# A 64-byte tile ahead of the retention heads' turned output

## The chip, the core and the metric

The kernel runs on one NeuronCore of a Trainium2 chip. Its engines work side by side, each with its own instruction queue: TensorE (PE in the profile, with its weight loads listed apart as PEld), VectorE (DVE), ScalarE (ACT) and GpSimd (POOL); SyncE (SP) only issues DMAs. SBUF, the on-chip memory, has 128 partitions, and a tile of shape [128, ...] takes the same bytes in every partition. PSUM receives what TensorE computes. The metric is the device time of one execution in microseconds; of several executions the median is given.

## What is computed

One layer of a decoder trunk on 512 tokens and 16 learned meta tokens, D = 1024. One input projection feeds a retention branch (4 heads, values 512 wide) and a GLA branch (4 heads, values 256 wide); each branch is projected back to 1024 columns, weighted by a learned sigmoid gate and added; an output projection, the residual and a final RMS norm follow. Cut to what matters here:

```
u = rms_norm(h, norm_gain)
(rq, rk, rv, rg, gq, gk, gv, gg, glr, m_ret, m_gla) = jnp.split(u @ w_in, points, axis=-1)
o_ret = retention_chunked(rope(rq), rope(rk) * RET_QK_DIM ** -0.5, rv)
o_ret = head_group_norm(o_ret, ret_norm_gain) * jax.nn.silu(rg)
...
merged = jax.nn.sigmoid(m_ret) * (o_ret @ w_branch_ret) + jax.nn.sigmoid(m_gla) * (o_gla @ w_branch_gla)
h = h + merged @ w_out
return rms_norm(h, final_norm_gain)[:, N_META:]
```

The part that the change touches is `o_ret @ w_branch_ret`: per head a [1024 x 512] by [512 x 512] product.

## The kernel before

**Numbers in two parts.** Every matrix is held as a high and a low part in float32r (`hi` by a ScalarE cast, `lo` by a VectorE subtraction, both in `split`, L154), and a product is three matmuls: high by high, high by low, low by high (`mm3`, L188 to L193). In `nc.tensor.matmul(out, a, b)` the second argument `a` is the stationary operand, loaded into the array as weights ahead of the matmul, and `b` is the moving operand, streamed through it. The profile names them in the other order: `br_p<-oh,br_h` is the result, the moving tile, the stationary tile.

**Projections.** `quad` computes a pair of column blocks by a Strassen-like scheme of seven products of 24 matmuls each, mostly 256 columns wide; its matmuls are on L318. Weights come by DMA into six raw buffers, are split, and are held in three `hi` and three `lo` buffers of the pool `wp`.

**Retention heads.** For each head h the program runs `ret_qk`, `ret_g`, `ret_v`, `ret_scores` and `ret_attention(h)`. The last computes the four row blocks (`values`, `av` in the profile), norms and gates them, and turns them with TensorE transposes: `turn` (L478 to L493) writes the turned output, scaled by a gain, as the tiles `oh` (ScalarE, L491) and `ol` (VectorE, L492), each [128, 4, 512]. They are taken on L1331 and L1332: for heads 0, 1 and 2 from the pool `rp` under the tags `oh` and `ol` (one buffer each, so the three heads use the same bytes one after the other), for head 3 from the pool `cp`.

**Who reads them.** `branch` (L463 to L476) multiplies heads 0 and 1 with their rows of `w_branch_ret`: eight column blocks, in each 4 row blocks x 3 = 12 matmuls with 512 columns, 96 in a head. They alternate with the products of `quad` for the gate `mg` (`turns`, L1450). `ret_branches` (L1415 to L1441) takes heads 2 and 3 together, in two halves; in each half come first 48 matmuls of head 2 and then 48 of head 3, which add to the same PSUM banks. In all of them `oh` or `ol` is the moving operand and a `hi` or `lo` buffer the stationary one. Later the tags `oh` and `ol` hold `fgb` and `hs[1]` (L1491, L1492), which no matmul reads.

**Order.** Each engine's order is not simply that of the source: the build sorts instructions by when they are ready in its own estimate, with a few orders fixed by hand (`after`, `pin`). Waits between engines and for a buffer that becomes free are put in by the framework.

**Where tiles lie.** The built program gives each tile a byte offset in the partition. The last column is the offset's remainder by 128, which is 0 or 64 for all of these:

| tile | operand of | offset | mod 128 |
|---|---|---|---|
| `oh`, heads 0 to 2 | `br`, moving | 212,864 | 0 |
| `ol`, heads 0 to 2 | `br`, moving | 221,056 | 0 |
| `oh`, head 3 | `br`, moving | 4,800 | 64 |
| `ol`, head 3 | `br`, moving | 22,208 | 64 |
| the six `hi` and `lo` buffers of `wp` | `br`, stationary | 102,848 to 123,328 | 64 |
| `vh`, `vl` | `av`, moving | 173,952, 182,144 | 0 |
| `sh`, `sl` | `av`, stationary | 198,528, 203,648 | 0 |
| `ga12` (GLA branch) | `bg_a`, moving | 149,632 | 0 |
| fourth sum of `merged` (high, low) | last `wo_b`, stationary | 52,672, 70,080 | 64 |

Rows within these tiles lie multiples of 128 bytes apart, so the remainder holds for every matmul of the groups named. `oh` and `ol` of heads 0 to 2 are the last tiles of `rp`: `ol` ends at 229,248 of 229,376 bytes. Where `oh` begins, the GLA stage had held `ga22h` (tag `gQ`), a matmul operand of its last branch product.

Of the kernel before, what the change touches and what calls it, by code (L numbers as in the profile page):

```python
# [21 lines left out]
F32 = mybir.dt.float32  # L22
# [6 lines left out]
P = 128  # L29
# [79 lines left out]
def hybrid_kernel(ctx: ExitStack, tc: tile.TileContext, I, out: bass.AP):  # L109
    nc = tc.nc  # L110
# [39 lines left out]
    def pat(name):  # L150
        return pa.tile([P, 512], F32, tag="pa", name=name)
# [36 lines left out]
    def mm3(o, lh, ll, rh, rl, first, last, dense=False):  # L188
        m = nc.tensor.matmul(o, lh, rh, start=first, stop=False)  # L189
        if dense:  # L190
            pin(m)
        nc.tensor.matmul(o, lh, rl, start=False, stop=False)  # L192
        m = nc.tensor.matmul(o, ll, rh, start=False, stop=last)  # L193
        if dense:
            order[:] = [m]

    def rstd_of(x, n, rows, name, eps=EPS):
        v = sp.tile([P, 1], F32, tag="rv", name=f"{name}_v")
        r = sp.tile([P, 1], F32, tag="rr", name=f"{name}_r")
        nc.vector.tensor_scalar(v[:rows], x, 1.0 / n, eps, op0=ALU.mult, op1=ALU.add)  # L200
        R["pow"] = nc.gpsimd.tensor_tensor(r[:rows], v[:rows], mhalf[:rows], op=ALU.pow)
        return r
# [275 lines left out]
    def turn(src, half, oh, ol, gain, gcol, name):  # L478

        for e2 in range(2):  # L480
            pt = pat(f"{name}_{half}{e2}")
            for e in range(2):
                for b in range(2):
                    nc.tensor.transpose(pt[:, (2 * e + b) * P:(2 * e + b + 1) * P],
                                        src[:, 2 * half + b, (2 * e2 + e) * P:(2 * e2 + e + 1) * P], ident)
            for e in range(2):
                k = 2 * e2 + e
                g = gain[:, gcol + k:gcol + k + 1]
                v = pt[:, 2 * e * P:(2 * e + 2) * P]
                h = oh[:, k, half * 256:(half + 1) * 256]  # L490
                nc.scalar.activation(h, v, AF.Copy, scale=g)  # L491
                nc.vector.scalar_tensor_tensor(ol[:, k, half * 256:(half + 1) * 256], v, g, h.bitcast(F32),  # L492
                                               op0=ALU.mult, op1=ALU.subtract)  # L493
# [701 lines left out]
    rp = ctx.enter_context(tc.tile_pool(name="rp", bufs=1, reuse_waits="tile"))  # L1195
# [6 lines left out]
    def tmp(name):  # L1202
        return rp.tile([P, 2 * HT], F32, tag="tmp", name=name, bufs=7)[:, :512]
# [122 lines left out]
    def ret_attention(h):  # L1326
        sh, sl, sm = R["s", h]
        vh, vl = R["v", h]
        vm, sg = R["vm", h], R["sg", h]

        oh, ol = [(rp if h < 3 else cp).tile([P, 4, T], F32R, tag=f"o{n}" if h < 3 else f"x{n}0", name=f"o{n}{h}")  # L1331
                  for n in "hl"]  # L1332
        R["o", h] = oh, ol

        def values(ib):
            ps = pat(f"av{h}{ib}")
            for jb in range(ib + 1):
                o = SOFF[jb] + (ib - jb) * P
                mm3(ps, sh[:, o:o + P], sl[:, o:o + P], vh[:, jb, :], vl[:, jb, :], jb == 0, False)
            nc.tensor.matmul(ps, sm[:, ib * P:(ib + 1) * P], vm, start=False, stop=True)  # L1340
            b6 = sp.tile([P, 6], F32, tag="b6", name=f"b6{h}{ib}")
            mv = sp.tile([P, 2], F32, tag="mv", name=f"mv{h}{ib}")
            nc.vector.bn_stats(b6, ps)
            nc.vector.bn_aggr(mv, b6)
            r = rstd_of(mv[:, 1:2], 1.0, P, f"g{h}{ib}")
            nm = sp.tile([P, 1], F32, tag="nm", name=f"nm{h}{ib}")
            nc.vector.scalar_tensor_tensor(nm, mv[:, 0:1], -1.0, r, op0=ALU.mult, op1=ALU.mult)
            on = tmp(f"on{h}{ib}")
            nc.scalar.activation(on, ps, AF.Identity, scale=r, bias=nm)
            nc.vector.tensor_mul(sg[:, ib, :], on, sg[:, ib, :])  # L1350

        for ib in range(NTB):
            values(ib)
            R["pow", h] = R["pow"]
            yield
        if h < 2:
            yield
        for half in range(2):
            turn(sg, half, oh, ol, rgain, h * 4, f"ot{h}")
            yield  # L1360
# [82 lines left out]
    for h in range(4):  # L1443
        if h == 0:
            drain(ret_qk(h))
        else:
            at = ret_attention(h - 1)
            weave(ret_qk(h), at if h < 3 else islice(at, NTB + 1))
        if h % 3:
            weave(turns(gates_gla(h - 1), ret_branch(h - 1)), ret_rope(h), skip=2)  # L1450
            weave(ret_g(h), ret_scores(h))
            drain(ret_v(h))
        else:
            weave(run(ret_g(h), ret_v(h)), run(every(ret_rope(h), 3, 2, at if h else None), ret_scores(h)))
    weave(gates_ret(), ret_attention(3))

    mh, ml = [[cp.tile([P, 4, T], F32R, tag=f"x{n}1", name=f"m{n}0"),
# [150 lines left out]
```

## Time and profile before

| | |
|---|---|
| median of 3 runs (lowest, highest) | 763.93 us (763.68, 764.01) |
| span of the profiled execution | 762.2 us |
| busy share: PE, PEld, DVE, ACT, POOL | 98%, 92%, 80%, 59%, 17% |
| granted TensorE clock, mean | 0.996 |
| DMA | 116.89 MB, 153 GB/s on the mean |

The profiled execution's own time is not given apart from its span; between the span and the median lie 1.7 us. A PE row's duration includes the pipeline, so neighbouring matmuls overlap in the profile; how fast they follow each other is read from the starts of rows, or from a piece of the chain of waits, which counts each stretch of time once. The windows below name times from the span's start.

### The profile page before, as it was taken

The page shows a single profiled execution, that of the slowest core. Times are in us where ns is not written, and L with a number is a line of the kernel's source. Part 1 is how long each engine was busy: PE and PEld are TensorE (multiplying, and loading weights), DVE is VectorE, ACT ScalarE, POOL GpSimd, SP SyncE. Part 2 cuts the span into 40 slices and gives each one's busy share as a digit, 9 for nine tenths or more (in the row PEclk, how much of TensorE's full clock was granted, in tenths as well). Part 3 has the DMA queues.
Part 4 walks back from the last instruction along what each step waited for, and adds up shares of the span by engine and source line. Part 5 has one row for each costly group of instructions (what it writes and reads, how often), then busy time and mean ns, then how long its engine had stood idle before and what let it go on. Part 6 is the DMA issues. An engine that isn't in the chain of part 4 may idle for free.

```text
span 762.2 us, 14057 instructions
## 1 busy us (share of the span) xinstructions
PE 750.4 (98%) x5595; PEld 701.5 (92%) x5595; DVE 611.2 (80%) x873; ACT 451.2 (59%) x764; POOL 133.4 (17%) x172
## 2 busy tenths in 40 slices
PE   9999999999989999999999999999999999999996
PEld 6799899999989999998889999889999999988996
DVE  6799877689897799778957688876787989775994
ACT  7897584666974465545646455555554756532562
POOL 2211200112231122110330100240002210111142
PEclk9999999999999999999999999999999999999999
DMA  9864321822568973753684563696477357687503
GB/s 301 277 146 106 89 84 45 185 82 70 137 168 229 295 171 91 164 144 119 176 239 125 117 161 111 166 206 154 120 166 159 93 148 193 227 196 199 136 29 111
DMA packets 99995, 116.89 MB, mean 153 GB/s; under 512 B 5717, under 2 KB 90837, under 8 KB 99673
## 3 DMA queue, kind: packets, MB, share of 16 engines
q1 hardware_dynamic: 79896, 88.19, 37.8%
q0 software_dynamic: 19744, 27.27, 19.6%
q8 instruction: 44, 0.72, 0.4%
q10 hardware_dynamic: 288, 0.53, 0.2%
q14 instruction: 23, 0.18, 0.1%
HBM read 104.44 MB, written 11.53 MB: 152 GB/s over the span
## 4 chain that ended last, share of the span: by engine, by line
PE 87%; DVE 9%; issue 2%; ACT 1%; POOL 0%; POOLq 0%; DVEq 0%
PE rv_b L318 6%; PE rg_b L318 6%; PE rqk_b L318 5%; PE rqk_c L318 4%; PE br_p L192 4%; PE br_p L193 3%; PE br_p L189 3%; PE gg_b L318 3%; PE mr_b L318 3%; PE gv_p L640 3%; PE rv_c L318 3%; PE bg_b L318 3%; PE rg_c L318 3%; PE mg_b L318 2%; PE gg_c L318 2%
## 5 line engine op out<-in xcount | busy, mean ns | idle before, releaser
L192 PE MATMUL br_p<-ol,br_h 128*128 128x512 f32 x128 | 50.6, 395 | 1.7 <-DVE ol L492 1.7
L189 PE MATMUL br_p<-oh,br_h 128*128 128x512 f32 x128 | 50.4, 394 | 0.0
L193 PE MATMUL br_p<-oh,br_l 128*128 128x512 f32 x128 | 50.3, 393 | 0.0
L154 ACT CAST rv_h<-rv_w 128x1024 fp32r<-128x1024 f32 x24 | 25.2, 1052 | 26.9 <-DVE rv_w L371 9.6
L154 DVE TENSOR_TENSOR rv_l<-rv_w,rv_h 128x1024 fp32r<-128x1024 f32 x24 | 29.3, 1221 | 9.2 <-ACT rv_h L154 9.2
L154 DVE TENSOR_TENSOR rg_l<-rg_w,rg_h 128x1024 fp32r<-128x1024 f32 x20 | 24.4, 1219 | 8.4 <-ACT rg_h L154 8.4
L192 PEld LDWEIGHTS br_p<-ol,br_h 128*128 128x128 f32 x128 | 24.0, 188 | 7.4 <-DVE ol L492 2.4
L154 ACT CAST br_h<-br_w 128x1024 fp32r<-128x1024 f32 x16 | 16.8, 1050 | 23.4 <-PE br_p L192 9.9
L282 POOL DMA_DIRECT2D rqk_x<-in_w_in_dram x8 | 10.4, 1305 | 109.5 <-DVE vl L154 66.2
L193 PEld LDWEIGHTS br_p<-oh,br_l 128*128 128x128 f32 x128 | 24.0, 188 | 5.5
L154 ACT CAST rg_h<-rg_w 128x1024 fp32r<-128x1024 f32 x20 | 21.0, 1052 | 13.2 <-PE br_p L192 5.0
L189 PEld LDWEIGHTS br_p<-oh,br_h 128*128 128x128 f32 x128 | 24.0, 188 | 5.1 <-ACT oh L491 0.2
L318 PE MATMUL rv_b<-rv_l,fh 128*128 128x256 f32 x96 | 27.1, 282 | 0.1
L318 PE MATMUL rqk_b<-fh,rqk_h 128*128 128x256 f32 (+1 forms) x96 | 27.2, 283 | 0.0
L318 PE MATMUL rqk_b<-fh,rqk_l 128*128 128x256 f32 (+1 forms) x96 | 27.1, 282 | 0.0
L318 PE MATMUL rqk_b<-fl,rqk_h 128*128 128x256 f32 (+1 forms) x96 | 27.1, 282 | 0.0
L154 DVE TENSOR_TENSOR rqk_l<-rqk_w,rqk_h 128x1024 fp32r<-128x1024 f32 x20 | 24.4, 1220 | 3.3 <-ACT rqk_h L154 3.3
L318 PE MATMUL rg_b<-rg_h,fl 128*128 128x256 f32 x96 | 27.0, 281 | 0.0
L318 PE MATMUL rv_b<-rv_h,fl 128*128 128x256 f32 x96 | 27.0, 281 | 0.0
L318 PE MATMUL rg_b<-rg_h,fh 128*128 128x256 f32 x96 | 26.9, 281 | 0.0
L318 PE MATMUL rg_b<-rg_l,fh 128*128 128x256 f32 x96 | 26.9, 281 | 0.0
L318 PE MATMUL rv_b<-rv_h,fh 128*128 128x256 f32 x96 | 26.9, 280 | 0.0
(720 smaller groups left out, 3239.4 us busy)
## 6 DMA issues: line engine op xcount, KB each, us to landing
rv_w<-in_w_in_dram SPq DMA_DIRECT2D x16, 512.0 KB, 4.2
br_w<-in_w_branch_ret_dram SPq DMA_DIRECT2D x16, 512.0 KB, 3.5
rqk_w<-in_w_in_dram SPq DMA_DIRECT2D x12, 512.0 KB, 4.5
rg_w<-in_w_in_dram SPq DMA_DIRECT2D x12, 512.0 KB, 5.4
rqk_x<-in_w_in_dram SPq DMA_DIRECT2D x8, 512.0 KB, 5.3
rqk_x<-in_w_in_dram POOLq DMA_DIRECT2D x8, 512.0 KB, 8.1
rg_x<-in_w_in_dram SPq DMA_DIRECT2D x8, 512.0 KB, 4.2
rg_x<-in_w_in_dram POOLq DMA_DIRECT2D x8, 512.0 KB, 7.7
```

The costliest lines, as they stand in the source:

```text
L154: return nc.scalar.copy(hi, src), nc.vector.tensor_sub(lo, src, hi.bitcast(F32))
L189: m = nc.tensor.matmul(o, lh, rh, start=first, stop=False)
L192: nc.tensor.matmul(o, lh, rl, start=False, stop=False)
L193: m = nc.tensor.matmul(o, ll, rh, start=False, stop=last)
L282: x = nc.gpsimd.dma_start(t, block(0, 1), accum_op=ALU.add)
L318: m = nc.tensor.matmul(ps[t][:, :n] if wide else ps[t], l, r, start=first and j == 0, stop=kk == 3 and j == 2, skip_group_check=not fresh ...
L640: m = nc.tensor.matmul(pss[t], (al if j == 1 else ah)[t // 2, kh][:, k, c], (lo if j == 2 else hi)[:, kk, :], start=q == kk == j == 0, sto ...
```

## The change

Ahead of the two tiles of head 0, a tile of 16 floats, 64 bytes in each partition, is taken from the same pool and set to zero on GpSimd. Nothing reads it. Tiles of a pool follow one another in the order in which their tags first appear, so `oh` begins at 212,928 and `ol` at 221,120 for heads 0, 1 and 2 (remainder 64 by 128), and `ol` ends at 229,312. No other tile moves.

```
         vm, sg = R["vm", h], R["sg", h]
 
+        if h == 0:
+            nc.gpsimd.memset(rp.tile([P, 16], F32, name="gap"), 0.0)
         oh, ol = [(rp if h < 3 else cp).tile([P, 4, T], F32R, tag=f"o{n}" if h < 3 else f"x{n}0", name=f"o{n}{h}")
                   for n in "hl"]
         R["o", h] = oh, ol
```

More of the change, by code (lines that the diff above doesn't have):

```diff
@@ L1329, in ret_attention @@
         vm, sg = R["vm", h], R["sg", h]
+        if h == 0:
+            nc.gpsimd.memset(rp.tile([P, 16], F32, name="gap"), 0.0)
         oh, ol = [(rp if h < 3 else cp).tile([P, 4, T], F32R, tag=f"o{n}" if h < 3 else f"x{n}0", name=f"o{n}{h}")
```

## The prediction, made before the result was known

> **What bounds the kernel now.** I read the page's busy shares first, then its chain of waits, then the groups.
>
> ```profile
> span 762.2 us, 14057 instructions
> ...
> PE 750.4 (98%) x5595; PEld 701.5 (92%) x5595; DVE 611.2 (80%) x873; ACT 451.2 (59%) x764; POOL 133.4 (17%) x172
> ...
> PE 87%; DVE 9%; issue 2%; ACT 1%; POOL 0%; POOLq 0%; DVEq 0%
> ...
> L192 PE MATMUL br_p<-ol,br_h 128*128 128x512 f32 x128 | 50.6, 395 | 1.7 <-DVE ol L492 1.7
> L189 PE MATMUL br_p<-oh,br_h 128*128 128x512 f32 x128 | 50.4, 394 | 0.0
> L193 PE MATMUL br_p<-oh,br_l 128*128 128x512 f32 x128 | 50.3, 393 | 0.0
> ```
>
> TensorE is busy for 98% of the span and holds 87% of the chain that ended last. So what counts is how closely its matmuls follow each other. The three `br` groups are the only matmuls that read the moved tiles: 3 x 128, of which heads 0, 1 and 2 have 288. Their mean durations are alike and tell nothing, since rows overlap; the starts do. From the timeline of PE, the first matmul of each run of 48 in the last stage, which by the code takes head 2, head 3, head 2, head 3, and the first matmul after them:
>
> ```profile
> 668.49 0.40 PE L189 MATMUL br_p<-oh,br_h 128*128 128x512 f32 x1
> ...
> 679.69 0.39 PE L189 MATMUL br_p<-oh,br_h 128*128 128x512 f32 x1
> ...
> 690.59 0.39 PE L189 MATMUL br_p<-oh,br_h 128*128 128x512 f32 x1
> ...
> 701.79 0.39 PE L189 MATMUL br_p<-oh,br_h 128*128 128x512 f32 x1
> ...
> 712.69 0.28 PE L189 MATMUL wo_p<-wo_h,mh 128*128 128x256 f32 x1
> ```
>
> The runs take 11.20, 10.90, 11.20 and 10.90 us. Shape, weights' buffers and stage are the same; head 2 needs 11.20 / 48 = 233.3 ns a matmul, head 3 only 227.1. What the code makes different is the moving tile: head 2's lies at remainder 0 by 128 bytes and head 3's at 64, like the weights. Heads 0 and 1, whose blocks of 12 alternate with products of 24, show head 2's pace. From the chain of waits (start, length, what):
>
> ```profile
> 358.83 2.85 PE mg_a L318 x24
> ...
> 364.49 2.84 PE mg_b L318 x24
> ...
> 484.33 2.81 PE mg_b L318 x24
> ...
> 489.94 2.81 PE mg_c L318 x24
> ```
>
> Between the pieces lie 364.49 - 361.68 = 2.81 us for head 0 and 489.94 - 487.14 = 2.80 us for head 1, each for 12 matmuls: 234 and 233 ns.
>
> Is it the match of the two remainders, or merely head 3's place? The `av` matmuls (512 columns too) have both operands at remainder 0, moving tile high up in SBUF. Timeline of PE, the first of 13 in a row and the last:
>
> ```profile
> 338.47 0.39 PE L189 MATMUL av<-vh,sh 128*128 128x512 f32 x1
> ...
> 341.19 0.39 PE L1340 MATMUL av<-vm,sm 128*128 128x512 f32 x1
> ```
>
> 2.72 us over 12 intervals is 226.7 ns. So 0 with 0 (`av`) and 64 with 64 (head 3) run at 227; 0 with 64 (heads 0 to 2) runs at 233. For 256 columns the sign is the other one. Chain of waits, `bg_a` (0 with 64) and the last `wo_b` (64 with 64):
>
> ```profile
> 244.02 2.72 PE bg_a L318 x24
> ...
> 741.95 2.88 PE wo_b L318 x24
> ```
>
> These are 113.3 and 120 ns. All four paces are whole multiples of 6.67 ns: 34 and 18 where the remainders match, 35 and 17 where they don't. My reading, which nothing here proves: the moving stream and the next weight load step through blocks of 64 bytes in turn, so a steady pace is an even number of steps with matching remainders and an odd number otherwise; 512 columns need at least 34 and 256 at least 17.
>
> **The change part by part.** *The moved tiles.* `oh` and `ol` of heads 0 to 2 go to remainder 64, that of the weights. I take 226.7 ns for their matmuls, the pace of `av`, also head 3's but for the changeover. Bounds: 226.7, the fastest steady pace that the rows of this width show, and 233.3, no effect. A loss, as matching brings at 256 columns, is excluded by two matching pairs of this width, `av` and head 3. I take the lower end, that of the nearest rows: head 3's, in the same loop. The saving is 233.3 - 226.7 = 6.67 ns a matmul. For heads 0 and 1 the first matmuls can't gain, because they wait for `ol`. Chain of waits at head 1:
>
> ```profile
> 461.03 0.21 PE av L192
> ...
> 461.26 1.24 DVE rqk_l L154
> ...
> 476.06 0.48 DVE ol L492
> ...
> 476.58 0.50 PE br_p L192
> ```
>
> The wait is at the fifth matmul (the second `oh`, `ol` pair), so 92 of 96 gain: 2 x 92 x 6.67 = 1.23 us. Head 2 has 96 x 6.67 = 0.64 us, and where its runs change to head 3's, the latter take 10.90 instead of 48 x 226.7 = 10.88; twice 0.02 goes too. Sum: 1.90 us.
>
> *Does it reach the end?* VectorE is the path in three stretches after head 0's product: the one above, one at 606 to 620, and one from 704.7. If such a stretch began at a time of its own, TensorE would only wait longer. But the chain enters each from a matmul: `av` at 461.03 above, and
>
> ```profile
> 603.24 2.62 PE rg_b L318 x23
> ...
> 605.91 0.25 DVE ol L492
> ...
> 619.85 2.97 PE rv_b L318 x23
> ...
> 704.73 0.70 DVE sigr L1438
> ```
>
> The last begins with the product of `br_p` of head 3 in the second half, after all of head 2. So all terms lie ahead of what ends the span, and I let 1.90 us through. What comes late next: VectorE's stretch up to 476.5, which costs up to the 0.61 us of head 0 if it doesn't start earlier.
>
> *Writes to the moved tiles.* ScalarE and VectorE write both kinds of place already:
>
> ```profile
> L491 ACT ACTIVATE oh<-ot,rgain x32: 455/478/506, 348.6 to 668.2; 128x256 fp32r<-128x256 f32 x32
> L492 DVE SCALAR_TENSOR_TENSOR ol<-ot,rgain,oh x32: 467/472/478, 350.4 to 669.5; 128x256 fp32r<-128x256 f32 x32
> ```
>
> Head 3's 8 of 32 are among them, and VectorE's least and greatest are 11 ns apart: nothing.
>
> *The memset.* One GpSimd instruction; its nearest rows are memsets of 128x128 and 128x1 (lines view), 207 and 104 ns, and 64 bytes lie between. It waits until `ga22h` has been read for the last time. The rows of POOL there, that of `ga22h`'s matmuls (first and last start), and behind the first `rqk_x` a cast, the sum of weights and the product that reads it:
>
> ```profile
> L1187 POOL MEMSET stb<- 128x128 f32 x4 | 0.6, 207 | 0.0
> L124 POOL MEMSET mhalf<- 128x1 f32 x1 | 0.1, 104 | 0.0
> ...
> 243.99 1.30 POOL L282 DMA_DIRECT2D rqk_x<-in_w_in_dram  x1 [11.43 <-DVE bg_l L154]
> 250.19 1.29 POOL L282 DMA_DIRECT2D rqk_x<-in_w_in_dram  x1 [4.90 <-DMA rqk_x<-in_w_in_dram]
> 250.94 0.87 POOL L1201 MEMSET km<- 128x256 f32 x1
> 263.65 1.29 POOL L282 DMA_DIRECT2D rg_x<-in_w_in_dram  x1 [11.84 <-issue]
> ...
> L318 PE MATMUL bg_c<-ga22h,bg_h x16: 279/280/280, 229.8 to 251.8; 128*128 128x256 f32 x16
> 252.25 1.05 ACT L154 CAST rqk_h<-rqk_w 128x1024 fp32r<-128x1024 f32 x1 [1.77 <-PE bg_c L318]
> 253.08 1.23 DVE L371 TENSOR_TENSOR rqk_w<-rqk_w,rqk_x 128x1024 f32<-128x1024 f32 x1 [1.35 <-DMA rqk_x<-in_w_in_dram]
> ...
> 260.86 2.90 PE rqk_b L318 x24
> ```
>
> POOL idles from 251.81 to 263.65, just behind the memset of `km`, which likewise waits for a GLA tile; `gap` may run from 252.1, where the last row of `ga22h` ends (251.8 and 0.28). I take nothing, hidden by these 11.84 us; behind it stands only the `rg_x` issue at 263.65. Were the cover gone, it would cost its 0.1 to 0.2 us.
>
> **Sum.** 762.2 - 1.9 = 760.3 us of span. The three runs' median is 1.7 us above the span shown, which I leave as it is: 763.93 - 1.90 = **762.0 us**.
>
> **The rivals.** *The place doesn't matter (0.08).* Then 763.9. Besides the remainder, head 3's tiles lie low in SBUF and farther apart, and a saving that hung on that wouldn't come. Against it: `av` reaches 226.7 from high up, with `vh` and `vl` as far apart as `oh` and `ol`. The Trainium skill's page "TensorE: Matmul & The Clock Gate", section "Step-by-step: what each phase is for", speaks for this rival: loading the next weights takes no read bandwidth from the running matmul, since TensorE has two read ports; by that rule 763.9 stays. The trace's 11.20 and 10.90 us for the same 48 matmuls don't agree with it.
>
> *The saving is lost in a later wait (0.17).* If VectorE's stretches hang on DMAs after all, heads 0 and 1 lose what they gained and only head 2's 0.68 remains: 763.3. Against it: the chain enters them from matmuls.
>
> *The memset holds POOL (0.07, slower).* Orders come from readiness, as `km`'s memset shows: it stands ahead of `rqk`'s loads in the source and runs behind them. If `gap` goes ahead of the first `rqk_x` at 243.99, that DMA leaves at 252.3, 8.3 us later. The sum at 253.08, which already waits for it, then ends at 262.6 instead of 254.3; a cast of 1.05 us and a split, which VectorE does in about the 1.23 of the sum, put its product at 264.9 at best, against 260.86: 4.0 us of stall. 763.93 - 1.90 + 4.0 = 766.0. It decides only if the memset is ahead of that issue; between the two issues the delay is 2.1 us, for a buffer used later. Against it: `km`'s memset was put behind both, and `gap` comes later in the source.
>
> *More than the sum (0.06).* The waits at heads 0 and 1 shrink too, or the order shifts in its favour: 761.2.
>
> **How the numbers follow.** Forecast 0.62, rivals 0.08, 0.17, 0.07, 0.06. A measurement here can tell about 0.2%, 1.53 us, so faster means below 762.40 and slower above 765.46. Of the forecast's 0.62, 0.60 lies below 762.40 and 0.02 above, where a few tenths are lost. Faster: 0.60 + 0.06 = 0.66. Same: 0.02 + 0.08 + 0.17 = 0.27. Slower: 0.07. The range runs from 761.4 to 764.0: it takes in the forecast and the two cases without or with little gain, and leaves out the slower case and most of the larger gain. Both ends of the unknown pace lie in it: 226.7 ns gives the forecast, 233.3 the 763.9 of no effect; 0.2 us on either side are the spread of the three runs.
>
> **What would show it.** The four runs of 48 should all take 10.88 us, the 12 between `mg` products 2.72, `av` and `bg_a` what they do now, and the memset should stand behind 251.8 on POOL. I am wrong if head 2's runs still take 11.20; or if they take 10.88 and the waits on `ol` or `rv_l` have grown by as much; or if `rqk_x` leaves later than 244.

## The result and the profile after

The median is 762.89 us (762.25 to 763.14, 19 runs) against 763.87 us of the kernel before (763.40 to 764.66, 19 runs) on the same chip: ratio 0.9986, interval 0.9979 to 0.9992. That is about 1.0 us less, where 1.9 us had been forecast. The page of the kernel after, with the busy shares, the chain by engine and one of the three `br` groups:

```profile
PE 749.7 (98%) x5595; PEld 702.0 (92%) x5595; DVE 611.7 (80%) x873; ACT 451.0 (59%) x764; POOL 133.4 (18%) x173
...
PE 87%; DVE 9%; issue 2%; ACT 1%; POOL 0%; POOLq 0%; DVEq 0%
...
L192 PE MATMUL br_p<-ol,br_h 128*128 128x512 f32 x128 | 50.1, 392 | 1.7 <-DVE ol L492 1.7
```

The span is 761.3 us, 0.9 us shorter. TensorE holds the same 87% of the chain, and its idle time on `ol` is 1.7 us as before: no new wait took the saving. The order of the 5595 matmuls is unchanged. The timeline of PE, kernel after, at the same five places as in the prediction, and the eleventh matmul of the first run (start, duration, instruction):

```profile
668.26 0.39 PE L189 MATMUL br_p<-oh,br_h 128*128 128x512 f32 x1
...
670.57 0.39 PE L192 MATMUL br_p<-ol,br_h 128*128 128x512 f32 x1
...
679.18 0.39 PE L189 MATMUL br_p<-oh,br_h 128*128 128x512 f32 x1
...
690.06 0.39 PE L189 MATMUL br_p<-oh,br_h 128*128 128x512 f32 x1
...
700.94 0.39 PE L189 MATMUL br_p<-oh,br_h 128*128 128x512 f32 x1
...
711.82 0.28 PE L189 MATMUL wo_p<-wo_h,mh 128*128 128x256 f32 x1
```

The four runs of 48 take 10.92, 10.88, 10.88 and 10.88 us. Before, head 2's took 11.20 and head 3's 10.90. The 192 matmuls need 43.56 us instead of 44.20: 0.64 us saved. What the first run has too much lies in its first ten matmuls: they take 670.57 - 668.26 = 2.31 us, 231 ns each, and the other 38 take 8.61 us, 226.6 ns each. This slow beginning is called an entry below.

For heads 0 and 1 it is different. Here are, from the chain of waits (start, length, what) and the timeline of PE, kernel before, VectorE's last piece on `ol` ahead of head 0's product, some pieces behind it, and the first matmul after all 96 of head 0 and after those of head 1 (head 1's `ol`, 476.06, stands in the prediction):

```profile
356.17 0.48 DVE ol L492
...
370.13 2.81 PE mg_c L318 x24
...
375.73 2.81 PE mg_b L318 x24
```

```profile
395.17 0.28 PE L318 MATMUL rg_b<-rg_h,xh 128*128 128x256 f32 x1
...
514.99 0.28 PE L318 MATMUL rg_b<-rg_h,xh 128*128 128x256 f32 x1
```

And the same of the kernel after:

```profile
356.34 0.49 DVE ol L492
...
370.19 2.84 PE mg_c L318 x24
...
375.80 2.85 PE mg_b L318 x24
381.40 2.83 PE mg_c L318 x24
386.95 2.84 PE mg_b L318 x24
...
476.00 0.49 DVE ol L492
```

```profile
395.11 0.28 PE L318 MATMUL rg_b<-rg_h,xh 128*128 128x256 f32 x1
...
514.75 0.28 PE L318 MATMUL rg_b<-rg_h,xh 128*128 128x256 f32 x1
```

From `ol` to the first matmul after the head, head 0 took 395.17 - 356.17 = 39.00 us and takes 38.77; head 1 took 38.93 and takes 38.75. Together that is 0.41 us, not 1.23. With head 2's 0.64 it makes 1.05 us, which is the measured gain within its interval. The span gained only 0.9, because the kernel after came to head 0's `ol` 0.17 us later, in a stretch that the change doesn't touch. So the sum closes, and one term of the forecast is too large by 0.8 us.

The pieces show where that went. The 12 `br` matmuls between 370.19 + 2.84 and 375.80 take 2.77 us, not 2.72; only some blocks, as the one from 384.23 to 386.95, reach 2.72. The starts in the block ahead of 370.19 show the same entry as in head 2's first run: ten matmuls take 2.31 us, and only the last two come at the full pace. And the product behind a block takes 2.84 instead of 2.81. A pair of 12 `br` and 24 `mg` lasts 375.80 - 370.19 = 5.61 us, against 5.60 before: the saving is given back at the borders between the two widths.

### The profile page after: what moved, and what is told of

It reads as the page before. It is cut to its first block, busy times and chain, and to the rows that moved or that the text cites. A ratio compares the mean times of both kernels' runs of the same rounds, so it can differ in the third digit from the quotient of the medians.

```text
span 761.3 us, 14058 instructions
## 1 busy us (share of the span) xinstructions
PE 749.7 (98%) x5595; PEld 702.0 (92%) x5595; DVE 611.7 (80%) x873; ACT 451.0 (59%) x764; POOL 133.4 (18%) x173
## 4 chain that ended last, share of the span: by engine, by line
PE 87%; DVE 9%; issue 2%; ACT 1%; POOL 0%; POOLq 0%; DVEq 0%
PE rv_b L318 6%; PE rg_b L318 6%; PE rqk_b L318 5%; PE rqk_c L318 4%; PE br_p L192 3%; PE br_p L193 3%; PE br_p L189 3%; PE gg_b L318 3%; PE mr_b L318 3%; PE gv_p L640 3%; PE rv_c L318 3%; PE bg_b L318 3%; PE rg_c L318 3%; PE mg_b L318 2%; PE gg_c L318 2%
```

## The experiments

**Two questions** were put to the chip. Is it the remainders of the two addresses that count, and by 128? And where did the 0.8 us of heads 0 and 1 go: to the entries into each block (theory A), or to whatever feeds TensorE there, so that a faster pace only waits elsewhere (rival B)? All runs, with the ratio to the kernel before and its interval; the columns h2 and h3 give the first run of 48 of head 2 and of head 3 in the last stage, read from the timeline as above. The runs below the kernel after come from three chips, where the kernel before had a median of 764.00 (e1 to e4), 763.87 (e5, e6, y, x) and 763.66 us (e7 to e9, z), so ratios are to be compared, not medians:

| run | median us | ratio (interval) | span | h2 us | h3 us |
|---|---|---|---|---|---|
| kernel after | 762.89 | 0.9986 (0.9979, 0.9992) | 761.3 | 10.92 | 10.88 |
| e1_ol_alone | 764.14 | 1.0003 (0.9994, 1.0012) | 762.0 | 11.24 | 10.92 |
| e2_gap_behind | 764.05 | 1.0001 (0.9992, 1.0010) | 762.2 | 11.20 | 10.90 |
| e3_head3_moved | 762.96 | 0.9991 (0.9982, 0.9999) | 761.4 | 10.92 | 11.01 |
| e4_gap32 | 764.33 | 1.0004 (0.9995, 1.0013) | 763.0 | 11.19 | 10.88 |
| e5_block_nogap | 775.46 | 1.0149 (1.0135, 1.0163) | 773.7 | 11.20 | 10.90 |
| e6_block_gap | 776.03 | 1.0150 (1.0128, 1.0171) | 773.7 | 10.92 | 10.88 |
| y_weights64 | 763.13 | 0.9992 (0.9983, 1.0001) | 761.2 | 11.15 | 11.21 |
| x_pitch | 766.22 | 1.0033 (1.0021, 1.0046) | 764.4 | 11.19 | 10.90 |
| e7_head3_128 | 763.46 | 0.9996 (0.9987, 1.0005) | 761.7 | 10.92 | 11.20 |
| e8_twos_nogap | 764.67 | 1.0010 (1.0001, 1.0019) | 762.5 | 11.20 | 10.90 |
| e9_twos_gap | 763.05 | 0.9989 (0.9980, 0.9998) | 761.2 | 10.92 | 10.88 |
| z_merged64 | 762.41 | 0.9981 (0.9972, 0.9989) | 760.5 | 10.92 | 10.88 |

### Is it the memset, or the move? (e2_gap_behind)

The same tile and memset, but behind the two lines that take `oh` and `ol`, so that these stay where they were:

```
-        if h == 0:
-            nc.gpsimd.memset(rp.tile([P, 16], F32, name="gap"), 0.0)
         oh, ol = [(rp if h < 3 else cp).tile([P, 4, T], F32R, tag=f"o{n}" if h < 3 else f"x{n}0", name=f"o{n}{h}")
                   for n in "hl"]
+        if h == 0:
+            nc.gpsimd.memset(rp.tile([P, 16], F32, name="gap"), 0.0)
```

> The zeroed 64-byte tile is taken behind oh and ol: one more GpSimd instruction as in the changed kernel, but oh and ol stay at remainder 0 by 128. Theory (the match of the remainders sets the pace): as before, 763.9 us within 0.4, head 2's runs of 48 matmuls 11.20 us, head 3's 10.90. Rival (the memset and what it does to the order of work brings the gain): 762.9 us, with head 2's runs still 11.20.

The ratio is 1.0001, and the first run of 48 of head 2 takes 11.20 us as before. The extra instruction brings and costs nothing that an interval of 0.1% on either side would show. So the effect comes from the move.

### One of the two tiles alone (e1_ol_alone)

```
...
         for n in "hl":
+            if h == 0 and n == "l":
+                nc.gpsimd.memset(rp.tile([P, 16], F32, name="gap"), 0.0)
             t = (rp if h < 3 else cp).tile([P, 4, T], F32R, tag=f"o{n}" if h < 3 else f"x{n}0", name=f"o{n}{h}")
...
```

> The 64-byte tile is taken between oh and ol: oh stays at remainder 0, ol goes to 64. Of three matmuls in a row one matches its weights and two don't. Theory with a price for each change between match and mismatch: hardly a gain, head 2's runs 11.1 to 11.2 us, 763.7 to 764.1 us. Rival (each matmul has its own pace, nothing carries over): a third of the matmuls gain 6.67 ns, head 2's runs 11.2 - 0.11 = 11.09 us, and a third of the changed kernel's gain, 763.5 us.

Head 2's 48 take 11.24 us, more than with both tiles at the old place (11.20), although a third of them now run at the fast place. If each matmul had a price of its own, a third of 48 x 6.67 ns would have gone, 0.11 us. So the pace is that of a sequence and not of each matmul. It is a first sign that changes between the two kinds cost, though this run doesn't price them one by one.

### Half the move (e4_gap32)

```
-            nc.gpsimd.memset(rp.tile([P, 16], F32, name="gap"), 0.0)
+            nc.gpsimd.memset(rp.tile([P, 8], F32, name="gap"), 0.0)
```

> The tile ahead of oh and ol has 32 bytes instead of 64, so they lie at remainder 32. Theory in its narrow form (steps of 64 bytes, a steady pace is a whole number of them): half a step off, head 2's runs lie between the two paces or at one of them, 10.88 to 11.20 us, and the time between 762.9 and 763.9. Rival (any move from remainder 0 helps, whatever its size): 10.88 and 762.9. A run above 11.20 would speak against both.

Head 2's first run takes 11.19 us, so that another place as such would help is excluded; for head 2, 32 bytes are as good as none.

### Head 3 out of step (e3_head3_moved)

The kernel after, with head 3's two tiles taken 64 bytes later (those of heads 0 to 2 are taken as before):

```
...
+            oh, ol = [cp.tile([P, 4 * T + 16], F32R, tag=f"x{n}0", name=f"o{n}3")[:, 16:]
+                      .rearrange("p (k t) -> p k t", k=4) for n in "hl"]
```

> The changed kernel, and head 3's two tiles begin 64 bytes later within their buffers, so they lie low in SBUF as before but at remainder 0. Theory (match): head 3's two runs of 48 now take 11.20 us each instead of 10.88, head 2's stay near 10.9; 0.64 us more than the changed kernel, 763.5 us. Rival (low in SBUF, or far apart, is what makes head 3 fast): head 3's runs stay at 10.88 and the time at 762.9.

Timeline of PE, starts of head 3 and of the next run of head 2:

```profile
678.94 0.40 PE L189 MATMUL br_p<-oh,br_h 128*128 128x512 f32 x1
...
689.95 0.40 PE L189 MATMUL br_p<-oh,br_h 128*128 128x512 f32 x1
```

Head 3 becomes slower at a place whose remainder differs from that of the weights, but only to 11.01 us (229 ns a matmul), not to 11.20. The direction was right and the size wrong. In the prediction's reading, two places by 128 can only match or not, and a mismatch has one pace. Here is a second one.

### The weights moved instead (y_weights64)

```
+    nc.gpsimd.memset(wp.tile([P, 16], F32, name="gap"), 0.0)
...
-    ss = sp.tile([P, NTB + 1], F32, tag="ss5", name="ss5", bufs=1)
+    ss = pad[:, 3:8]
```

The kernel before, with the gap ahead of the `hi` and `lo` buffers; the second edit, and one like it, give the 64 bytes back, so that none of the other tiles whose places are listed ahead of the prediction moves.

> No gap ahead of oh and ol; instead the six hi and lo buffers of the weights lie 64 bytes later (remainder 0). Then oh and ol of heads 0 to 2 match again (0 with 0), head 3's mismatch (64 with 0). Theory (it is the two remainders against each other that count, whichever operand moves): head 2's runs of 48 in the last stage take 10.88 us, head 3's 11.0 to 11.2, and of the 256-wide products those with moving remainder 0 go from 113.3 to 120 ns and those with 64 from 120 to 113.3, so bg_a's 24 take 2.88 instead of 2.72 and each pair of halves of the projections stays the same in sum. The kernel lies within 2 us of 764, since what br wins, bg_a, bg_b and bg_c lose. Rival (only where the moving tile lies counts): head 2 stays at 11.20, head 3 at 10.90, bg_a at 2.72.

Timeline of PE, head 2, head 3, head 2; and `bg_a` in the chain of waits:

```profile
667.26 0.39 PE L189 MATMUL br_p<-oh,br_h 128*128 128x512 f32 x1
...
678.41 0.40 PE L189 MATMUL br_p<-oh,br_h 128*128 128x512 f32 x1
...
689.62 0.39 PE L189 MATMUL br_p<-oh,br_h 128*128 128x512 f32 x1
```

```profile
243.40 2.85 PE bg_a L318 x24
```

Half of the expectation failed. Head 3 slows to 11.21 us with its own tiles untouched, and `bg_a` slows from 2.72 to 2.85 us: so it is the two addresses against each other, whichever moves. But head 2, whose remainders by 128 now match, should take 10.88 and takes 11.15. By 128 this can't be understood.

### Rows at another pitch (x_pitch)

```
-HW = 272
+HW = 288
...
-        return wp.tile(list(shape), F32, tag="raw", name=name, bufs=6)
+        return wp.tile(list(shape), F32, tag="raw", name=name, bufs=5)
```

With the edits of y_weights64, and head 3's tiles 64 bytes later.

> As the run before, and the rows of the projections' input tiles lie 1152 instead of 1088 bytes apart, so that every 256-wide product of the projections has moving remainder 64 and stationary 0; head 3's oh and ol lie 64 bytes later (remainder 0); one raw buffer of six is given up for the room. Theory: the projections' products all take 24 x 113.3 = 2.72 us instead of 2.72 and 2.88 in turn, while head 2's and head 3's runs take 10.88 us each: up to 10 us less in sum where PE is the bound, less what the loss of a raw buffer and bg cost (bg about 1.6 us). I expect 753 to 765. Rival (the remainder doesn't matter at 256 columns, the difference between products comes from where they stand): the products stay at 2.80 to 2.85 on the mean, and the kernel is at 764 or slower by what the missing buffer costs.

Timeline of PE, head 2, head 3, head 2:

```profile
671.02 0.39 PE L189 MATMUL br_p<-oh,br_h 128*128 128x512 f32 x1
...
682.21 0.39 PE L189 MATMUL br_p<-oh,br_h 128*128 128x512 f32 x1
...
693.11 0.40 PE L189 MATMUL br_p<-oh,br_h 128*128 128x512 f32 x1
```

Heads 2 and 3 both have remainder 0 by 128 here, and so have the weights. Head 2 takes 11.19 us, head 3 10.90. That refutes the remainder by 128. By 256 the two differ: head 2's tiles lie at 128, head 3's and the weights at 0. The kernel as a whole became slower: the projections' products did not all come to 2.72 us, and DMA holds 4% of the chain that ended last, where the kernel before has none. That the lost raw buffer brought it there is likely but not shown, and how much each of the two costs was not separated.

Worked out by 256, as the moving tile's address less that of the weights, all runs fall in line. (Within each row of the table all the weights have the same remainder, so a matmul's own weights and the next can't be told apart.) In the kernel before, `oh` and `ol` of heads 0 to 2 lie at 128, the weights at 192, head 3's tiles at 192, and both operands of `av` at 128:

| difference by 256 | 512 columns, ns a matmul | from |
|---|---|---|
| 0 | 226.7 | `av`; head 3 before; heads 2 and 3 after; head 3 of x_pitch (at 0 and 0), but for entries |
| 64 | 229 | head 3 of e3 |
| 128 | 232 to 233 | head 2 of y and of x_pitch |
| 192 | 233.3 | head 2 before; head 3 of y |
| 224 | 233 | head 2 of e4 |

### By 128 or by 256? (e7_head3_128)

The kernel after, with head 3's two tiles taken 128 bytes later (those of heads 0 to 2 are taken as before):

```
...
+            oh, ol = [cp.tile([P, 4 * T + 32], F32R, tag=f"x{n}0", name=f"o{n}3")[:, 32:]
+                      .rearrange("p (k t) -> p k t", k=4) for n in "hl"]
```

> The changed kernel, with head 3's two tiles 128 bytes later (remainder 64 by 128 as before, but 64 instead of 192 by 256; the weights lie at 192 by 256). Theory 128 (what counts is whether both remainders by 128 are the same): head 3 stays at 2.72 us per 12 matmuls, and the kernel at the changed kernel's 762.9. Theory 256 (what counts is the moving address less that of the next stationary, by 256; the runs so far give 226.7 ns at 0, 229 at 64, 232 to 233 at 128 and 233.3 at 192): head 3's difference is 128, so its 12 take 2.78 to 2.80 us, its two runs of 48 some 11.1 to 11.2 us, and the kernel 0.5 to 0.6 us more, 763.4.

Timeline of PE, head 3 and the next run of head 2:

```profile
678.90 0.40 PE L189 MATMUL br_p<-oh,br_h 128*128 128x512 f32 x1
...
690.10 0.39 PE L189 MATMUL br_p<-oh,br_h 128*128 128x512 f32 x1
```

Head 3's run takes 11.20 us although its remainder by 128 is that of the weights. Theory 128 falls, and theory 256 stands. By the ratios (0.9996 and 0.9986) the kernel is about 0.8 us slower than the kernel after, where 0.5 to 0.6 had been expected; the two intervals overlap.

### The heads in one block (e5_block_nogap, e6_block_gap)

```
-            weave(turns(gates_gla(h - 1), ret_branch(h - 1)), ret_rope(h), skip=2)
+            weave(run(gates_gla(h - 1), ret_branch(h - 1)), ret_rope(h), skip=2)
```

The edit stands once in the kernel before and once in the kernel after.

> The kernel before, but the 96 branch products of head 0 (and of head 1) stand in one block ahead of the mg products and no longer alternate with them in twelves. Control for the next run. Both theories: the 96 take 96 x 233.3 ns = 22.4 us per head, as head 2 does without the gap. The kernel's time may be off by a few tenths to some us from 763.9, because DVE's work on the next head is met by other work of PE; only the difference to the next run is read.

> The changed kernel with the same block order. Theory A (the missing 0.4 us of each of heads 0 and 1 went into changeovers: each block of 12 that follows a 256-wide product takes about 43 ns more than 12 x 226.7, and the product behind it up to 40 ns more): in one block there is one changeover per head instead of eight, so a head takes about 21.8 us against 22.4, 0.6 us less, and with head 2 the kernel is 1.8 to 1.9 us faster than the run without the gap. Rival B (PE is held up there by what feeds it, so that a faster pace only waits elsewhere): the blocks shrink by 0.6 us but waits behind them grow, and the difference stays near the 1.0 us that the change itself brought.

The times decide nothing: both are 12 us slower and equal within their intervals. Part of the reading can be saved. Timeline of PE in head 0, 60 matmuls apart, without the gap and with it:

```profile
383.73 0.39 PE L189 MATMUL br_p<-oh,br_h 128*128 128x512 f32 x1
...
397.73 0.39 PE L189 MATMUL br_p<-oh,br_h 128*128 128x512 f32 x1
```

```profile
384.32 0.39 PE L189 MATMUL br_p<-oh,br_h 128*128 128x512 f32 x1
...
397.92 0.39 PE L189 MATMUL br_p<-oh,br_h 128*128 128x512 f32 x1
```

14.00 and 13.60 us are 233.3 and 226.7 ns: away from the borders, head 0 gains the whole 6.67 ns. A large part of what kept it from the time is in the windows view, in head 1 (stretch, length, PE busy and matmuls, then the other engines; the number behind POOL is the granted clock), first without the gap, then with it:

```profile
499.00:511.00 12.00, 8.74 (x32) 6.67 (x31) 7.55 (x11) 4.33 (x7) 3.73 (x4) 0.86 0.81 227
```

```profile
499.00:511.00 12.00, 8.74 (x28) 6.62 (x27) 7.37 (x10) 3.28 (x6) 3.73 (x4) 0.72 0.82 231
```

In this order TensorE waits for `br_l`, and the clock falls behind the wait. In the run with the gap it was lower here (0.72 against 0.86) and four matmuls fewer were done. Behind the wait the two runs are 0.09 us apart (502.86 and 502.95), and when both are at full pace again 1.11 us (507.55 and 508.66): in these two executions the clock took 1.0 us. The run with the gap had also come to head 0 0.6 us later, in a stretch where the two are the same.

### Blocks of 24 (e8_twos_nogap, e9_twos_gap)

```
+    def twos(gen):
+        for i, _ in enumerate(gen):
+            if i % 2:
+                yield
-            weave(turns(gates_gla(h - 1), ret_branch(h - 1)), ret_rope(h), skip=2)
+            weave(turns(gates_gla(h - 1), twos(ret_branch(h - 1))), ret_rope(h), skip=2)
```

The edit stands once in the kernel before and once in the kernel after.

> The kernel before, but heads 0 and 1 give two blocks of 12 branch products (24 matmuls) between two mg products instead of one. Control for the next run. Both theories: 24 of them take 24 x 233.3 = 5.60 us, an mg product behind them 2.80, and one behind another mg product 2.84.

> The changed kernel with the same order in twos. Theory A (the loss is paid per entry into a block, 0.04 us in its first 12 matmuls and 0.04 us in the mg product behind it): each run of 24 takes 2.76 + 2.72 = 5.48 us instead of 5.60 and the mg product behind it 2.84 instead of 2.80, so a pair gains 0.08 us net where the order in ones gained 0.00 to 0.04; four pairs in each of two heads and head 2 give together 1.1 to 1.3 us against the run without the gap. Rival B (the loss isn't at the entries but in what feeds PE): the runs of 24 stay above 5.52 us or waits come between them, and the difference is 1.0 or less.

Chain of waits in head 0, without the gap:

```profile
356.22 0.48 DVE ol L492
...
370.10 2.81 PE mg_b L318 x24
...
378.50 2.81 PE mg_c L318 x24
...
389.71 2.83 PE mg_c L318 x24
392.54 2.84 PE mg_b L318 x24
```

and with it:

```profile
355.62 0.48 DVE ol L492
...
369.31 2.84 PE mg_b L318 x24
...
377.63 2.85 PE mg_c L318 x24
...
391.63 2.84 PE mg_b L318 x24
```

Timeline of PE with the gap, behind head 1:

```profile
605.65 0.38 PE L318 MATMUL rg_c<-rg_l,xh 128*128 128x256 f32 x1 [0.34 <-DVE rg_l L154]
```

The 24 between two products take 378.50 - 372.91 = 5.59 us without the gap and 377.63 - 372.15 = 5.48 with it, as theory A had it, and no wait comes between them. A pair takes 8.40 and 8.32 us: 0.08 net, where the order in ones gained nothing. From `ol` to the last product of the head it is 36.32 and 36.01 us, so head 0 gains 0.31 us instead of the 0.23 of the order in ones. The spans differ by 1.3 us (762.5 and 761.2), the medians by 1.6. By the intervals of the two ratios alone, rival B's 1.0 us isn't excluded. In the pieces theory A holds inside the blocks, but the spans are no proof of it. Of their 1.3 us, 0.6 lies ahead of head 0's `ol` (356.22 and 355.62), where the two runs are the same. Up to the first matmul behind each head, heads 0 and 1 gain 0.35 and 0.38. By head 2's first matmul (668.83 and 668.13) 0.6 is gone again, about half of it in a wait for `rg_l`: the second matmul of `rg_c` comes 0.61 us behind the first (605.04 and 605.65) instead of 0.32. The last stage gives 0.64. So in this execution a part of what the blocks gained was waited away behind them, as rival B has it.

The row at 389.71 tells one thing more. Its product stands behind another `mg` product, not behind a `br` block, and takes 2.83 us, as they do in the kernel after. So 2.84 is the usual length, and 2.81 came with the old place of `oh` and `ol`. The slow pace alone doesn't bring it. Here is the chain of waits of e4_gap32, where head 0's matmuls are slow too:

```profile
370.62 2.84 PE mg_c L318 x24
...
376.26 2.84 PE mg_b L318 x24
```

The 12 between them take 376.26 - 373.46 = 2.80 us, and the products still 2.84. What makes a product shorter behind some blocks stays open.

### Using it elsewhere (z_merged64)

```
+    def later(n, tag, name):
+        return cp.tile([P, 4 * n + 16], F32R, tag=tag, name=name)[:, 16:].rearrange("p (k t) -> p k t", k=4)
...
-    mh, ml = [[cp.tile([P, 4, T], F32R, tag=f"x{n}1", name=f"m{n}0"),
+    mh, ml = [[later(T, f"x{n}1", f"m{n}0"),
...
-    sums = [[cp.tile([P, 4, 256], F32R, tag=f"f{n}{i}", name=f"ms{n}{i}") for i in range(3, 7)] for n in "hl"]
+    sums = [[later(256, f"f{n}{i}", f"ms{n}{i}") for i in range(3, 7)] for n in "hl"]
```

> The changed kernel, with ten tiles of the last projection (mh, ml of the first half and the sums ms), which are its stationary operands, 64 bytes later: the difference moving less next stationary, by 256, goes from 0 to 192 for 216 matmuls with 256 columns. Theory 256 (at 256 columns 0 gives 120 ns, 64 gives 117.7, 128 gives 119, 192 gives 113.3): the products wo_b take 2.72 us instead of 2.88, and 216 x 6.67 ns = 1.4 us go, at the end of the kernel where nothing can swallow them but the waits of its last sums: 761.5 against the changed kernel's 762.9, ratio to the kernel before 0.997. Rival (those products hang on their weights' DMAs and splits): the products get shorter but the waits between them grow, and 762.9 stays.

Chain of waits, kernel after, one of VectorE's pieces ahead of the last three products of `wo`, and the last of these:

```profile
730.54 1.13 DVE wo_l L154
...
741.07 2.88 PE wo_b L318 x24
```

The same product in the chain of waits of this run, and, on its timeline of PE, the first matmul of the projection:

```profile
740.59 2.73 PE wo_b L318 x24
```

```profile
711.40 0.28 PE L189 MATMUL wo_p<-wo_h,mh 128*128 128x256 f32 x1
```

The product `wo_b` falls from 2.88 to 2.73 us, as the difference of 192 gives. But the span falls by 0.8 us only, and 0.42 of this lies ahead of the projection, which begins at 711.40 instead of 711.82 although nothing ahead of it was changed. Such a difference is usual between executions: the four runs with the gap and the old order (kernel after, e3, e7 and this one) come to head 2's first matmul between 667.83 and 668.26. From the projection's beginning to the end it is 760.5 - 711.40 = 49.10 us against 49.48: 0.4 us of the 1.4. In the stretch around 730.54 the chain is VectorE's (`wo_l`), so what the products there gain is waited away; what comes behind can keep it. The rival is right for the larger part. The kernel beats the one before (ratio 0.9981). Against the kernel after (0.9986) the intervals overlap, so the times show no gain over it.

## Why the prediction was right, and where its size was wrong

*What bounds the kernel* held: the time went with the pace of the matmuls, at the same share of the chain, and no engine or wait took TensorE's place. From the first matmul behind head 0 to head 1's `ol` it is 80.89 us before and after; from the first behind head 1 to head 2's first it took 153.50 us (514.99 to 668.49) and takes 153.51 (514.75 to 668.26). So nothing was lost in VectorE's stretches there; that rival falls, and so does the one that the place doesn't matter. The rule of the Trainium skill that spoke for the latter (page "TensorE: Matmul & The Clock Gate", section "Step-by-step: what each phase is for": loading weights takes no read bandwidth from the running matmul) was read there as leaving 763.9 us; 762.89 and head 2's 10.92 us disagree with that reading. Whether the two operands contend for read bandwidth, no run shows. By the number alone the rival with the later wait couldn't be told from the forecast: 762.89 lies nearer to its 763.3 than to the forecast of 762.0. It also lies among the outcomes that the prediction had called the same (762.40 to 765.46, chance 0.27), and not faster (0.66). The range held it, but the gain is about half of the forecast.

*Head 2* was forecast at 0.64 us and 0.04 at the changes to head 3. It gave 0.64 in sum: the changes to head 3 are gone (10.88), but the entry into head 2's first run costs 0.04 (10.92).

*Heads 0 and 1* are the term that was mis-sized: 2 x 92 x 6.67 ns = 1.23 us, and 0.41 measured. The pace of 226.7 ns was taken for every matmul, from runs of 13 and 48, and the changes of width were put at nothing. Here a run has 12, and behind each the width changes. The entry costs up to 0.04 us of the 0.08 that a block gains, and the `mg` product behind loses 0.03 to 0.04. Between two products, blocks of 24 gained what this account says. The prediction had the row that warned of it: head 3's 10.90 instead of 10.88 behind head 2. It counted that change as a gain to come and didn't ask what the changes to and from the 256-wide products would cost.

*The reading by 128* was wrong, and gave the right answer by luck: the move by 64 bytes brings the difference by 256 from 192 to 0 as well, where another move to the same remainder by 128 would have left the slow pace, as e7 shows for head 3. With it falls the picture of even and odd numbers of steps: the paces of 229 and 232 ns (e3, y) are neither.

*The memset* ran where it was expected, behind that of `km` and between the issues of `rqk_x` and `rg_x`. Timeline of POOL, kernel after:

```profile
251.94 0.87 POOL L1201 MEMSET km<- 128x256 f32 x1
252.19 0.67 POOL L1332 MEMSET gap<- 128x16 f32 x1
```

Its row reads 0.67 us, not 0.1 to 0.2, but it overlaps the one of `km`, so it doesn't tell what the memset takes alone. POOL then idles for 9.42 us until the `rg_x` issue at 262.28, which hides it. The rival that it holds POOL falls.

**What stays open:** why entering a run costs 0.04 us in some blocks and nothing in others, why some products behind are shorter, whether a matmul's own weights or the next count, and by what mechanism the two addresses meet. The runs show the dependence on the difference by 256, not its cause.

## What to carry to other kernels

Where TensorE's matmuls follow each other without a wait and two groups of one shape differ in pace, compare the addresses of the moving tile and of the next weights before anything else; a gap of 64 bytes may be worth 3% of the pace. Count the pace only for runs of one width that are long against their entry, and price each change of width on its own: here up to half of what a block of 12 could gain went at its entry and most of the rest in the product behind. And a rule read from two values (0 and 64) fits more than one law; move each operand by several steps before it is used elsewhere.

## What the runs showed of the hardware

The pace of float32r matmuls follows the moving tile's address less the weights', by 256 bytes, in the runs of this case. At 512 columns 0 is best of the five differences that were run (226.7 ns, against 233.3 at 192). The figures for 64 and 128 are means: in e3's head 3 the starts lie about 226, 229 and 232 ns apart in turn, in e7's 229 and 238. At 256 columns the order turns round: 192 gives 2.72 us for 24 (`bg_a`, 113.3 ns), 128 gives 2.85 (`bg_a` of y_weights64) and 0 gives 2.88 (`wo_b`, 120 ns).

In the block order a wait of 3.26 us was followed by matmuls at half speed. Timeline of PE, e6_block_gap, head 1:

```profile
502.95 0.79 PE L193 MATMUL br_p<-oh,br_l 128*128 128x512 f32 x1 [3.26 <-DVE br_l L154]
503.54 0.63 PE L189 MATMUL br_p<-oh,br_h 128*128 128x512 f32 x1
503.97 0.63 PE L192 MATMUL br_p<-ol,br_h 128*128 128x512 f32 x1
```

The last two start 0.43 us apart instead of 0.227, and the full pace is back at 508.66. The Trainium skill's page "TensorE: Matmul & The Clock Gate", section "What's actually happening", gives at least one window of about 3.4 us, idle for the clock to fall to half and busy for it to rise again. The trace agrees with the half pace and with the rise, 5.7 us after the wait; the row's 3.26 us of idle time is a little short of the page's window.
